# Rows 4 to 6 in halves, other sizes of the last loads, and another engine that clears the semaphores, in a streamed sum of squared differences

## The chip, the cores and the metric

The kernel runs on one core of one Trainium2 chip. The metric is device time in microseconds (us) of one execution. A profile of one execution is beside it: the instructions of every engine with start and duration, the DMA packets, and the times at which each transfer raised its semaphore (its landing).

## The reference

```python
def setup_inputs():
    batch, dim = 1024, 4096
    return {
        "x": np.random.randn(batch, dim).astype(np.float32),
        "y": np.random.randn(batch, dim).astype(np.float32),
        "axis": -1,
    }

def reference(x, y, axis):
    return np.sum((x - y) ** 2, axis=axis).astype(np.float32)
```

Two arrays of 16 MiB are read, and 1024 numbers are written.

## The kernel before

**Tiling.** Each of the 128 partitions holds 8 whole rows of x and of y, one after the other: 8 x 4096 = 32,768 columns (`xv`, `yv`, L60 and L61). The text calls them row 0 to row 7. X and Y have room in SBUF for six rows (`H = 6 * D`, L65), so columns from 24,576 on are put where rows 0 and 1 were (`home`, L97).

**Loads.** x comes in 6 pieces and y in 9, all issued by SP in one queue (`load`, L105 to L108), each with a semaphore of its own. The widths in columns stand in `xw` and `yw` (L72, L73). Two narrow pieces of y come last: the final `last` = 288 columns of row 7, and then the final `late` = 160 columns of row 3, which were left out of the first piece of y. `order` (L110 to L116) puts each piece of x ahead of the first piece of y that needs it. The first two loads are moved to the very start of the program (`early`). Loads up to column 24,576 are issued at once; the later ones wait on SP until the squares of rows 0 and 1 are done (L215) and are then all issued in a row (L219, L220). In the text x2 is the third piece of x, y8 the ninth piece of y; a column is one float on each of the 128 partitions.

**Work.** The loop at L191 goes through the pieces of y in the order of their loads. VectorE (DVE) waits until the piece and the x beside it have landed, and subtracts in place (`sub`, L168); a piece that crosses a row's end is cut there (`pieces_of`, L127). ScalarE (ACT) waits for the difference, squares it and adds it up along the row (`square`, L173). In the profile a square is two instructions, an ACTIVATE and an ACTIVATION_READ_ACCUMULATOR that writes the sum. Where a row is in several pieces, each sum goes into a column of `parts`, and `complete` (L181) adds them on DVE with a small TENSOR_REDUCE after waiting for ACT. Rows 0, 1, 2, 4 and 5 are squared whole and need none. Row 6 is in two parts and is completed after the fifth piece of y (`j == 4`, L221). Row 7 is in five parts and is completed last (L224). The late piece of row 3 (L197) is subtracted and then squared on DVE itself, in an instruction that starts from the partial sum that ACT left.

**End.** SP waits for all the sums and stores `results` (L226, L227). `close` then has SP clear the range of all the other semaphores (L44) while the store is under way, wait for the store's own semaphore, and take that semaphore back to zero in the same instruction (L45). Nothing follows it in the program.

Of the kernel before, what the change touches and what calls it, by code (L numbers as in the profile page):

```python
# [8 lines left out]
class Program:  # L9
# [27 lines left out]
        )  # L37
        self.entry[where:where] = taken

    def close(self, engine, stored, value):  # L40

        engine.sem_clear(range(self.sems[0].num, self.sems[-1].num + 1))  # L44
        engine.wait_ge(stored, value).then_inc(stored, -value)  # L45


def kernel(tc, x, y, axis, out):
    nc = tc.nc
    P = nc.NUM_PARTITIONS  # L50
    F32 = mybir.dt.float32
    Square = mybir.ActivationFunctionType.Square
    mult, add = mybir.AluOpType.mult, mybir.AluOpType.add

    B, D = x.shape
    R = B // P
    N = R * D


    xv = x.rearrange("(p r) d -> p (r d)", p=P)  # L60
    yv = y.rearrange("(p r) d -> p (r d)", p=P)  # L61
    ov = out.rearrange("(p r) -> p r", p=P)


    H = 6 * D  # L65
    X = nc.alloc_sbuf_tensor("X", [P, H], F32).ap()
    Y = nc.alloc_sbuf_tensor("Y", [P, H], F32).ap()
    results = nc.alloc_sbuf_tensor("results", [P, R], F32).ap()

    xw = [16384, 8192, 5568, 1824, 512, 288]  # L72
    yw = [16224, 8192, 2656, 2912, 928, 896, 512]  # L73
    late, last = 160, 288
    LATE = 3
    cut = (LATE + 1) * D - late
    assert sum(xw) == N and sum(yw) == N - late - last
    xs, c = [], 0
    for w in xw:
        xs.append((c, c + w))  # L80
        c += w
    ys, c = [], 0
    for w in yw:
        ys.append((c, c + w))
        c += w
        if c == cut:
            c += late
    ys += [(N - last, N), (cut, cut + late)]

    prog = Program(nc, tc)  # L90
    stored = nc.alloc_semaphore("stored")
    diffs = prog.semaphore("diffs")
    acts = prog.semaphore("acts")
    sums = prog.semaphore("sums")
    n = dict(diffs=0, acts=0, sums=0)

    def home(c0, c1):  # L97
        h0 = c0 % H
        return slice(h0, h0 + c1 - c0)


    landed_x, landed_y = [], []
    freed = []

    def load(landed, src, dst, name, c0, c1):  # L105
        sem = prog.semaphore("%s%d" % (name, len(landed)))
        nc.sync.dma_start(out=dst[:, home(c0, c1)], in_=src[:, c0:c1]).then_inc(sem, 16)  # L107
        landed.append(((c0, c1), sem))  # L108

    order = []  # L110
    have = 0
    for c0, c1 in ys:
        while have < c1:
            order.append((landed_x, xv, X, "x") + xs[len([o for o in order if o[3] == "x"])])
            have = order[-1][5]
        order.append((landed_y, yv, Y, "y", c0, c1))  # L116

    todo = list(order)
    for _ in range(2):
        load(*todo.pop(0))  # L120
    prog.early(mybir.EngineType.SP)
    while todo and todo[0][5] <= H:
        load(*todo.pop(0))


    row_parts = [[] for _ in range(R)]
    def pieces_of(c0, c1):  # L127
        pieces = []
        while c0 < c1:
            e = min(c1, (c0 // D + 1) * D)  # L130
            pieces.append((c0, e))
            c0 = e
        return pieces

    for c0, c1 in ys:
        for piece in pieces_of(c0, c1):
            row_parts[piece[0] // D].append(piece)
    parts, where = None, {}
    total = sum(len(p) for p in row_parts if len(p) > 1)
    parts = nc.alloc_sbuf_tensor("parts", [P, total], F32).ap()  # L140
    k = 0
    for r, p in enumerate(row_parts):
        for piece in p:
            where[piece] = parts[:, k : k + 1] if len(p) > 1 else results[:, r : r + 1]
            k += len(p) > 1
    first = {}
    k = 0
    for r, p in enumerate(row_parts):
        if len(p) > 1:
            first[r] = k  # L150
            k += len(p)

    def parts_of(r, m):
        return parts[:, first[r] : first[r] + m]

    seen_x = [0]

    def wait_loaded(c1, ysem):

        waits = []  # L160
        while seen_x[0] < len(xs) and xs[seen_x[0]][0] < c1:
            waits.append(seen_x[0])
            seen_x[0] += 1
        nc.vector.wait_ge(ysem, 16)
        for k in waits:
            nc.vector.wait_ge(landed_x[k][1], 16)

    def sub(c0, c1):  # L168
        a = X[:, home(c0, c1)]
        nc.vector.tensor_sub(out=a, in0=a, in1=Y[:, home(c0, c1)]).then_inc(diffs, 1)  # L170
        n["diffs"] += 1

    def square(c0, c1, acc):  # L173
        a = X[:, home(c0, c1)]
        nc.scalar.wait_ge(diffs, n["diffs"])
        nc.scalar.activation(out=a, in_=a, func=Square, accum_out=acc).then_inc(acts, 1)  # L176
        n["acts"] += 1

    squared = {}

    def complete(r):  # L181
        nc.vector.wait_ge(acts, squared[row_parts[r][-1]])
        nc.vector.tensor_reduce(  # L183
            out=results[:, r : r + 1],
            in_=parts_of(r, len(row_parts[r])),
            axis=mybir.AxisListType.X,
            op=add,
        ).then_inc(sums, 1)
        n["sums"] += 1

    for j, (c0, c1) in enumerate(ys):  # L191
        final = j == len(ys) - 1
        wait_loaded(c1, landed_y[j][1])
        for piece in pieces_of(c0, c1):
            sub(*piece)
            r = piece[0] // D
            if final:  # L197
                nc.vector.wait_ge(diffs, n["diffs"])
                nc.vector.tensor_tensor_reduce(  # L199
                    out=Y[:, home(*piece)],  # L200
                    in0=X[:, home(*piece)],
                    in1=X[:, home(*piece)],
                    scale=1.0,
                    scalar=parts_of(r, 1),
                    op0=mult,
                    op1=add,
                    accum_out=results[:, r : r + 1],
                ).then_inc(sums, 1)
                n["sums"] += 1
                continue  # L210
            square(*piece, where[piece])
            squared[piece] = n["acts"]
            if r in (0, 1):

                nc.sync.wait_ge(acts, n["acts"])  # L215
                while todo and todo[0][5] <= H + (r + 1) * D:
                    load(*todo.pop(0))
                if r == 1:
                    while todo:  # L219
                        load(*todo.pop(0))  # L220
        if j == 4:  # L221
            for r in (6,):
                complete(r)
    complete(7)  # L224

    nc.sync.wait_ge(sums, n["sums"])  # L226
    nc.sync.dma_start(out=ov, in_=results).then_inc(stored, 16)  # L227
    prog.close(nc.sync, stored, 16)


# [33 lines left out]
```

## Time and profile before

| what | value |
|---|---|
| median of 3 runs | 84.36 us (84.32 to 84.52) |
| the profiled execution's own time | 84.36 us |
| its span, first to last recorded instruction | 83.03 us (83.0 on the page) |
| outside the span | 1.33 us |
| DVE busy | 36.3 us (44%) in 18 instructions |
| ACT busy | 31.7 us (38%) in 27 instructions |
| DMA queue | 33.56 MB, busy for 95.2% of the span on 16 DMA engines |

The two compute engines are less than half busy, and the DMA queue nearly always. The page cuts the span into 40 slices and prints for each the busy share in tenths and the rate in GB/s. The chain of waits is followed back from the last instruction, and says at each step what released it. In the timeline each line gives the start, the duration, the engine, the source line, the operation with its shapes, and, in brackets, how long the engine stood idle before it and what ended that. A group such as "x3" runs from the start of the first to the end of the last of its instructions. SPq and POOLq are the sequencers of SyncE and GpSimd; their waits, drains and DMA issues aren't counted as busy.

### The profile page before, as it was taken

Reading aid. Unit: us, or ns where it says so; the run is one execution under the profiler, and the core shown is the slowest. Engines: PE = TensorE matmul, PEld = TensorE weight load, DVE = VectorE, ACT = ScalarE, POOL = GpSimd, SP = SyncE. Lnnn points to the kernel's source line nnn. Section 1 sums busy time; section 2 is a strip of 40 time slices with the busy share of each in tenths; the row PEclk is TensorE's granted clock in tenths of the full one; section 3 lists DMA queues with packets and bytes.
Section 4 is the critical chain, followed back from the end, with each engine's and each line's share of the span. In section 5 each row is a group of like instructions: output and inputs, shape, how many; then the busy total and the mean of one; then the engine's idle time right before and its main releaser. Section 6 shows DMA issues by size and latency. Waiting matters only on the chain.

```text
span 83.0 us, 109 instructions
## 1 busy us (share of the span) xinstructions
DVE 36.3 (44%) x18; ACT 31.7 (38%) x27; POOL 0.2 (0%) x4
## 2 busy tenths in 40 slices
DVE  0000000000000000000299999999099995979981
ACT  0500000000000000000001969798970796989991
POOL 0000000000000000000000000000000000000000
DMA  9299999929999997599799979979999999999940
GB/s 505 95 410 505 505 505 505 505 95 410 500 500 500 500 500 313 219 469 500 332 426 505 474 316 474 505 332 426 424 429 429 400 435 439 426 407 404 395 145 2
DMA packets 2304, 33.56 MB, mean 404 GB/s; under 512 B 384, under 2 KB 768, under 8 KB 1408
## 3 DMA queue, kind: packets, MB, share of 16 engines
q1 hardware_dynamic: 2304, 33.56, 95.2%
HBM read 33.55 MB, written 0.00 MB: 404 GB/s over the span
## 4 chain that ended last, share of the span: by engine, by line
DMA 68%; ACT 14%; DVE 14%; SPq 1%; issue 0%
DMA Y<-in_y_dram 68%; ACT X L176 14%; DVE X L170 14%; SPq L107 1%; DVE results L183 0%; SPq L215 0%
## 5 line engine op out<-in xcount | busy, mean ns | idle before, releaser
L170 DVE TENSOR_TENSOR X<-X,Y 128x4096 f32<-128x4096 f32 (+9 forms) x14 | 35.8, 2593 | 44.9 <-DMA Y<-in_y_dram 44.8
L176 ACT ACTIVATE X<-X 128x4096 f32<-128x4096 f32 (+8 forms) x13 | 29.7, 2288 | 47.7 <-DVE X L170 47.7
L176 ACT ACTIVATION_READ_ACCUMULATOR X<-X 128x1 f32 x13 | 2.4, 188 | 0.0
L176 ACT ACT_TABLE_LOAD x1 | 1.3, 1283 | 1.9 <-PEq L19 1.9
L183 DVE TENSOR_REDUCE results<-parts 128x1 f32<-128x2 f32 (+1 forms) x2 | 0.3, 154 | 0.2 <-ACT X L176 0.2
L199 DVE CUSTOM_DVE_ANT_0 Y<-X,parts 128x160 f32<-128x160 f32 x1 | 0.4, 385 | 0.0
L245 POOL MEMSET const-bfloat16-1.0<- 128x1 bf16 x1 | 0.1, 102 | 0.0
L245 POOL MEMSET const-uint8-127<- 128x1 uint8 x1 | 0.1, 102 | 0.0
L245 POOL MEMSET const-float32-0.0<- 128x1 f32 x1 | 0.1, 99 | 0.2 <-issue 0.2
L245 POOL MEMSET const-float32-1.0<- 128x1 f32 x1 | 0.1, 99 | 0.0
L199 DVE DVE_READ_ACCUMULATOR2_ANT results<- 128x1 f32 x1 | 0.1, 83 | 0.0
## 6 DMA issues: line engine op xcount, KB each, us to landing
Y<-in_y_dram SPq DMA_DIRECT2D x1, 8112.0 KB, 40.4
X<-in_x_dram SPq DMA_DIRECT2D x1, 4096.0 KB, 48.7
Y<-in_y_dram SPq DMA_DIRECT2D x1, 4096.0 KB, 58.0
X<-in_x_dram SPq DMA_DIRECT2D x1, 2784.0 KB, 13.4
Y<-in_y_dram SPq DMA_DIRECT2D x1, 1456.0 KB, 19.2
Y<-in_y_dram SPq DMA_DIRECT2D x1, 1328.0 KB, 16.2
X<-in_x_dram SPq DMA_DIRECT2D x1, 912.0 KB, 21.0
Y<-in_y_dram SPq DMA_DIRECT2D x1, 464.0 KB, 21.6
```

Of the source, the lines that this page charges most:

```text
L107: nc.sync.dma_start(out=dst[:, home(c0, c1)], in_=src[:, c0:c1]).then_inc(sem, 16)
L170: nc.vector.tensor_sub(out=a, in0=a, in1=Y[:, home(c0, c1)]).then_inc(diffs, 1)
L176: nc.scalar.activation(out=a, in_=a, func=Square, accum_out=acc).then_inc(acts, 1)
L183: nc.vector.tensor_reduce(out=results[:, r : r + 1], in_=parts_of(r, len(row_parts[r])), axis=mybir.AxisListType.X, op=add,).then_inc(sums, 1)
L199: nc.vector.tensor_tensor_reduce(out=Y[:, home(*piece)], in0=X[:, home(*piece)], in1=X[:, home(*piece)], scale=1.0, scalar=parts_of(r, 1), ...
L245: nc = _bacc.Bacc("TRN2", target_bir_lowering=False, num_devices=1)
```

## The change

Three things change. The pieces 1 to 4 of y, which hold rows 4, 5 and 6 and the first part of row 7, are subtracted and squared in two halves for each row that they touch. Rows 4 and 5 so have two partial sums each, and are completed beside row 6 at `j == 4`. The loads have other widths: the first piece of y is 32 columns wider, and the loads from row 6 on are 13 in place of 11 and narrower towards the end. And `close` no longer uses SP: GpSimd (POOL) waits for the store's semaphore, and then clears all the kernel's semaphores, that one among them. In the built program POOL's part is a drain that waits, followed by the clear.

```diff
-    def close(self, engine, stored, value):
-        engine.sem_clear(range(self.sems[0].num, self.sems[-1].num + 1))
-        engine.wait_ge(stored, value).then_inc(stored, -value)
+    def close(self, sem, value):
+        self.nc.gpsimd.wait_ge(sem, value)
+        self.nc.clear_and_free_semaphores(self.sems)
...
-    xw = [16384, 8192, 5568, 1824, 512, 288]
-    yw = [16224, 8192, 2656, 2912, 928, 896, 512]
-    late, last = 160, 288
+    xw = [16384, 8192, 5472, 1280, 960, 320, 160]
+    yw = [16256, 8192, 2624, 2784, 1344, 480, 480, 288]
+    late, last = 128, 192
     LATE = 3
+    halved = (1, 2, 3, 4)
...
-    stored = nc.alloc_semaphore("stored")
     diffs = prog.semaphore("diffs")
     acts = prog.semaphore("acts")
     sums = prog.semaphore("sums")
+    stored = prog.semaphore("stored")
...
-    def pieces_of(c0, c1):
+    def pieces_of(j, c0, c1):
         pieces = []
         while c0 < c1:
             e = min(c1, (c0 // D + 1) * D)
+            if j in halved:
+                h = (c0 + e) // 64 * 32
+                pieces.append((c0, h))
+                c0 = h
             pieces.append((c0, e))
             c0 = e
         return pieces
...
         if j == 4:
-            for r in (6,):
+            for r in (4, 5, 6):
                 complete(r)
     complete(7)

     nc.sync.wait_ge(sums, n["sums"])
     nc.sync.dma_start(out=ov, in_=results).then_inc(stored, 16)
-    prog.close(nc.sync, stored, 16)
+    prog.close(stored, 16)
```

The order of the last loads, with widths in columns, is:

| | order from row 6 on |
|---|---|
| before | x2 5568, y2 2656, y3 2912, x3 1824, y4 928, y5 896, x4 512, y6 512, x5 288, y7 288, y8 160 |
| after | x2 5472, y2 2624, y3 2784, x3 1280, y4 1344, x4 960, y5 480, y6 480, x5 320, y7 288, x6 160, y8 192, y9 128 |

On DVE there are 21 subtractions in place of 14 and 4 reductions in place of 2; on ACT 20 squares in place of 13; on SP 17 loads in place of 15.

More of the change, by code (lines that the diff above doesn't have):

```diff
@@ L133, in pieces_of @@
         return pieces
-    for c0, c1 in ys:
-        for piece in pieces_of(c0, c1):
+    for j, (c0, c1) in enumerate(ys):
+        for piece in pieces_of(j, c0, c1):
             row_parts[piece[0] // D].append(piece)
@@ L193 @@
         wait_loaded(c1, landed_y[j][1])
-        for piece in pieces_of(c0, c1):
+        for piece in pieces_of(j, c0, c1):
             sub(*piece)
```

## The prediction

> **What bounds the kernel now.** I read the page first, then the chain of waits, then the timeline of the last 5 us.
>
> ```profile
> DMA  9299999929999997599799979979999999999940
> ## 4 chain that ended last, share of the span: by engine, by line
> DMA 68%; ACT 14%; DVE 14%; SPq 1%; issue 0%
> ```
>
> The loads run to slice 39 of 40, and only the end is not theirs. The chain of waits says what hangs behind them:
>
> ```profile
> 70.12 2.94 DVE X L170
> ...
> 73.07 8.29 ACT X L176 x14
> ...
> 81.39 0.16 DVE results L183
> ```
>
> From 73.07 to 81.37 ACT squares without a pause: the tail's bound is ACT running late, not the last load. ACT was late since the whole-row squares of rows 4 and 5. The timeline's end:
>
> ```profile
> 79.28 1.43 DVE L170 TENSOR_TENSOR X<-X,Y 128x512 f32<-128x512 f32 x3 [0.16 <-DMA Y<-in_y_dram]
> 79.29 0.94 ACT L176 ACTIVATE X<-X 128x896 f32<-128x896 f32 x1
> ...
> 80.22 0.61 ACT L176 ACTIVATE X<-X 128x512 f32<-128x512 f32 x1
> ...
> 80.84 0.43 ACT L176 ACTIVATE X<-X 128x288 f32<-128x288 f32 x1
> 81.06 0.08 DVE L199 DVE_READ_ACCUMULATOR2_ANT results<- 128x1 f32 x1
> 81.17 0.19 ACT L176 ACTIVATION_READ_ACCUMULATOR X<-X 128x1 f32 x1
> 81.39 0.16 DVE L183 TENSOR_REDUCE results<-parts 128x1 f32<-128x5 f32 x1 [0.25 <-ACT X L176]
> 81.58 0.35 SPq L227 DMA_DIRECT2D out_dram<-results  x1
> ```
>
> DVE is through at 81.14 and waits 0.25 us for ACT. So at most 0.25 is won by a punctual ACT alone; more needs an earlier DVE. The store is issued at 81.58 and lands at 83.00 (1.42 later); SP's last wait ends the span at 83.03. The clear is hidden meanwhile:
>
> ```profile
> L44 SPq EVENT_SEMAPHORE_RANGE_CLEAR  x1: 62/62/62, 82.0 to 82.0; - x1
> L45 SPq EVENT_SEMAPHORE  x1: 17/17/17, 83.0 to 83.0; - x1
> ```
>
> I work from the profiled execution, 84.36 us: span 83.03 and 1.33 outside it, which I hold equal. It is also the median of the 3 runs.
>
> **Prices.** DVE, start to start without a wait between: 4.341 us for 4096 columns (60.327 to 64.670 unrounded: 4.343), 1.576 for 1440, so 0.077 + 0.00104 per column. ACT: 2.416 for 2656, 0.613 for 512, so 0.182 + 0.000841 per column. A difference reaches ACT 0.12 after DVE could start its next subtraction (64.67 to 64.79). A landing releases DVE 0.02 later.
>
> **Part 1, the loads.** Each of 16 DMA engines takes 8 of a load's 128 rows. Packets of 65,536 bytes take 2,418 ns, those of 640 bytes 32 ns: 0.0368 ns a byte, and with 4 x 8 bytes a column 1.177 ns a column. Between y1's landing (60.30) and y8's (80.20) lie 16,544 columns, 19.47 us by that price; the remaining 0.43 over 11 loads is 0.04 a load. After: y1 lands at 60.34 (32 columns more in y0), then 16,512 columns, 19.43, and 13 loads, 0.51: the last landing is 80.28, 0.08 later. By loads: y2 69.99, y3 73.32, y4 76.47, y5 78.23, y6 78.83, y7 79.61, y8 80.08, y9 80.27. Bounds of a load's fixed cost: 0.01 (y8 before: 0.20 after y7, of which its 160 columns are 0.19) and that whole 0.20; two extra loads cost 0.02 to 0.40. I take 0.08, since eleven rows give it.
>
> ```profile
> Y<-in_y_dram SPq DMA_DIRECT2D x1, 80.0 KB, 15.4
> ```
>
> This is y8, issued 15.4 us ahead of its landing. SP's issues are held up (4.87 us at most, y7), so two more could end about 10 us after the present 67.56, which is before their data's turn at 80; the store behind them on SP waits until 81 anyway.
>
> [...]
>
> **Part 2, the halves.** Seven more subtractions (0.077 each, 0.54) and squares (0.182 each, 1.27) lie mostly in idle time: before, DVE waits 1.03 for y2 and 0.57 for y3, ACT 3.02 for row 4. DVE after: rows 4 and 5 start at 60.36, 62.57, 64.78, 66.99 and end by 69.2, before y2. Row 6: 70.01 and 71.45; y3's four pieces 73.34 to 76.55, y4's two to 78.10. There the three completions stand, in front of y5 on DVE; each costs 0.065 (77.972 to 78.037 before). Row 6's last square starts at 75.14 and is done at 76.05, so none waits. y5 78.30, y6 78.87, y7 79.63 (landing), y8 80.11 (landing), y9 80.38.
>
> ACT then follows each half: row 5's second half starts at 69.32 and ends at 71.3 (72.83 before), row 6 71.57 and 73.01, y3 from 74.30, y4 77.44 and 78.22, y5 78.99, y6 79.58, y7 80.16, y8 80.58. That one takes 0.182 + 0.161, and 0.107 more until the accumulator is in (81.170 + 0.187 + 0.010 before): 81.03.
>
> DVE's own end: y9's 128 columns from 80.38, next possible start 80.59, its difference back at itself 0.12 later (80.71), the multiply 0.143 + 0.133 until the accumulator read at 80.99 (before 80.749 to 81.059 for 160), 0.065 to the next: 81.05. So both engines meet at 81.05 where before ACT alone gave 81.39: **minus 0.34**. The store is issued at 81.24 and lands at 82.66. The eight partial sums instead of five cost the last reduction nothing I can see (149 and 158 ns for 2 and 5).
>
> [...]
>
> **Part 3, the close.** SP ends with the store's issue. POOL has waited since 1.81 with nothing behind but the clear, and this now stands after the landing. The trace before has no clear on POOL; the nearest rows:
>
> ```profile
> L19 POOLq DRAIN  x2: 34/38/41, 1.2 to 1.5; - x2
> ```
> ```profile
> L245 POOLq DRAIN  x1: 181/181/181, 0.3 to 0.3; - x1
> ```
>
> Waking 0.017 as SP's, a drain 0.04, 0.08 between sequencer instructions (POOL's waits at 1.383 and 1.462), a clear 0.062 as SP's: 0.20, less SP's 0.034: **plus 0.17**. Below: 0.045, if drain and gap overlap the wait. Above: POOL's three rounds of start-up barriers, 1.06 to 1.81, 0.75 us for its whole routine, if ending on POOL costs something outside the span too. I take 0.17, nearest to the sequencer rows.
>
> Sum: 84.36 - 0.34 + 0.17 = **84.19 us** (82.86 span).
>
> **Rivals.**
> - Cheap close (0.045): 84.36 - 0.34 + 0.05 = 84.07. For it: the clear itself is 62 ns on SP. Against: POOL's drains take 4 to 5 times SP's 7 ns.
> - Loads dear: 0.40 for two, 0.32 more than I took: 84.51. Against: the rows between x2 and y8 show it nowhere.
> - The halves don't bring ACT forward (if DVE's additional work pushes every difference back): with whole pieces and the new loads the same sum gives ACT 81.44 and the reduction 81.46, +0.07: 84.36 + 0.07 + 0.17 = 84.60.
> - Slower: POOL as last engine costs its 0.75: 84.36 - 0.34 + 0.75 = 84.77. It decides from 0.34 on. For it: POOL idles from 1.81 and its end is hidden now, whatever it costs; against: its single instructions take 17 to 41 ns.
>
> **Numbers.** What a measurement can tell here is about 0.3%, 0.25 us: below 84.11 is faster, above 84.61 slower. Chances: forecast 0.45 (84.05 to 84.40), cheap close 0.17, loads dear 0.12, halves void 0.08, dear close 0.18. Faster: cheap close and 0.06 of the forecast, 0.23. Slower: dear close and nearly half of halves void, 0.21. Within: 0.56. The range leaves out most of the dear close, so 83.95 to 84.65.
>
> **What would show it.** Right: the last reduction starts at 81.0 to 81.1, ACT idles between squares after 71, the last load lands near 80.28, POOL's clear ends some 0.2 after the store's landing. Wrong: ACT busy without gap from 73 on; DVE unable to start y7 at its landing; the last landing beyond 80.4; or the time outside the span grown above 1.33, which would be POOL's end.

## The result: 0.6% slower, and the span unchanged

| | before | after |
|---|---|---|
| median of 4 runs | 84.42 us (84.32 to 84.52) | 84.91 us (84.87 to 85.03) |
| ratio after to before, 95% interval | | 1.0060 (1.0043 to 1.0078) |
| profiled execution, own time | 84.36 | 84.87 |
| its span | 83.03 | 83.04 |
| outside the span | 1.33 | 1.83 |

The change costs half a microsecond, and the last row alone holds it: the first and last instruction of the profile are as far apart as before. The profile of after follows, in the order of the lines shown before the change. First its page:

```profile
DMA  9289999948999997499899969989999999999940
...
DMA 64%; SPq 17%; DVE 12%; ACT 4%; issue 1%
```

The loads still run to slice 39. In the chain ACT has gone from 14% to 4%. (The 17% of SPq are SP's held-up load issues, 4.78 us at most, which the chain now follows back; SP issues its last load by 70.88, and that load lands at 80.37, so they delay nothing.) The chain of waits of after ends so (start, duration, what):

```profile
80.19 0.02 issue
80.21 0.57 DVE X L177 x2
80.78 0.03 issue
80.81 0.35 DVE Y L206
81.16 0.01 DVE results L206
81.17 0.14 DVE results L190
```

Where 8.29 us of ACT stood, there now stands DVE from the landing of y8 on. The timeline of after at the same place:

```profile
78.34 2.42 DVE L177 TENSOR_TENSOR X<-X,Y 128x480 f32<-128x480 f32 x5
...
80.67 0.35 ACT L183 ACTIVATE X<-X 128x192 f32<-128x192 f32 x1
...
80.92 0.19 ACT L183 ACTIVATION_READ_ACCUMULATOR X<-X 128x1 f32 x1
81.08 0.08 DVE L206 DVE_READ_ACCUMULATOR2_ANT results<- 128x1 f32 x1
81.14 0.16 DVE L190 TENSOR_REDUCE results<-parts 128x1 f32<-128x8 f32 x1
81.33 0.35 SPq L234 DMA_DIRECT2D out_dram<-results  x1
```

ACT's last sum is in at 81.11, just ahead of DVE's; the last reduction carries no idle time in brackets, where 0.25 us of waiting for ACT stood. It starts at 81.14, 0.25 ahead of before, in an execution whose loads landed 0.17 later (80.37 against 80.20). Then comes the close (line, duration min/median/max in ns, first and last start in us):

```profile
L46 POOLq DRAIN  x1: 88/88/88, 82.8 to 82.8; - x1
L46 POOLq EVENT_SEMAPHORE_RANGE_CLEAR  x1: 157/157/157, 82.9 to 82.9; - x1
```

The store lands at 82.74, the clear ends at 83.04: 0.30 us where SP needed 0.03. That eats the 0.25 of the tail. The other 0.50 lies after the last instruction, where the page shows nothing. The traces' record of semaphore updates reaches further. Its first update behind the span's end comes 0.14 after it before, at 83.171, and 0.53 after it in the changed kernel, at 83.564. The last update of semaphore 96 stands at 83.627 before, 0.60 after the span's end, and at 84.146 after, 1.11 after the span's end. Counted from the first instruction, the execution's own time is up 0.73 and 0.72 later. So 0.39 of the half microsecond lies between the program's last instruction and the first update behind it, and all of it ahead of that update of semaphore 96.

### The profile page after: what moved, and what is told of

The parts are those of the page before. It is cut to its first block, busy times and chain, and to the rows that moved or that the text cites. A ratio compares the mean times of both kernels' runs of the same rounds, so it can differ in the third digit from the quotient of the medians.

```text
span 83.0 us, 135 instructions
## 1 busy us (share of the span) xinstructions
DVE 36.8 (44%) x27; ACT 33.4 (40%) x41; POOL 0.2 (0%) x4
## 4 chain that ended last, share of the span: by engine, by line
DMA 64%; SPq 17%; DVE 12%; ACT 4%; issue 1%
DMA Y<-in_y_dram 64%; SPq L109 17%; DVE X L177 11%; ACT X L183 4%; DVE Y L206 0%; DVE results L190 0%; SPq L222 0%; DVE results L206 0%
## 5 line engine op out<-in xcount | busy, mean ns | idle before, releaser
L177 DVE TENSOR_TENSOR X<-X,Y 128x2048 f32<-128x2048 f32 (+10 forms) x21 | 36.2, 1779 | 44.4 <-DMA Y<-in_y_dram 44.3
L183 ACT ACTIVATE X<-X 128x2048 f32<-128x2048 f32 (+9 forms) x20 | 31.2, 1560 | 45.8 <-DVE X L177 45.7
L183 ACT ACTIVATION_READ_ACCUMULATOR X<-X 128x1 f32 x20 | 3.7, 187 | 0.0
```

## The experiments

My theory was that POOL, when it is the engine that ends last, costs the half microsecond. The rivals were the larger program (135 instructions in the trace against 109), and a clear that comes after the landing, on whatever engine. Each run is compared with runs of the kernel before on its own chip; "outside" is the profiled execution's time less its span. The diffs show the lines that matter; "..." stands for lines that add or move a semaphore, change the call of `close`, or put SP's close back.

**The new close alone**, on the kernel before.

```diff
-        engine.sem_clear(range(self.sems[0].num, self.sems[-1].num + 1))
-        engine.wait_ge(stored, value).then_inc(stored, -value)
+        self.nc.gpsimd.wait_ge(sem, value)
+        self.nc.clear_and_free_semaphores(self.sems)
...
```

> The kernel before with the new close alone. In the changed kernel the close took 0.26 us more inside the span (0.30 from landing to end against 0.03) and the time outside the span was 0.50 longer (1.83 against 1.33). Theory POOL-last (whatever POOL does last after the store costs 0.5 outside the span): 84.42 + 0.26 + 0.50 = 85.2, outside 1.83. Theory larger program (135 instructions against 109 cost the 0.5): 84.42 + 0.26 = 84.7, outside 1.33. Theory late clear (a clear of semaphores after the landing costs 0.5 outside, on any engine): 85.2, as POOL-last.

Measured: 85.29 against 84.57, ratio 1.0088 (1.0068 to 1.0109), outside 1.84. The larger program falls: this one has the loads and pieces of before.

**Halves and loads alone**: the changed kernel with SP's close.

```diff
-        self.nc.gpsimd.wait_ge(sem, value)
-        self.nc.clear_and_free_semaphores(self.sems)
+        engine.sem_clear(range(self.sems[0].num, self.sems[-1].num + 1))
+        engine.wait_ge(stored, value).then_inc(stored, -value)
...
```

> The changed kernel with the close of before on SP: halves and new loads alone. POOL-last and late clear: 84.91 - 0.76 = 84.15, outside 1.33, the last reduction near 81.14 as in the changed kernel. Larger program: 84.91 - 0.26 = 84.65, outside 1.83.

Measured: 84.22 against 84.57, ratio 0.9959 (0.9943 to 0.9974), outside 1.33, the last reduction at 81.15:

```profile
81.15 0.16 DVE L190 TENSOR_REDUCE results<-parts 128x1 f32<-128x8 f32 x1
```

By its ratio it is the fastest kernel of this study, ahead of before and of after. The effects of the two runs, +0.88% and -0.41%, add up to +0.47%; the whole change gave +0.60% (0.43 to 0.78).

**Only the wait on POOL**, with SP's clear under the store.

```diff
         engine.sem_clear(range(self.sems[0].num, self.sems[-1].num + 1))
-        engine.wait_ge(stored, value).then_inc(stored, -value)
+        self.nc.gpsimd.wait_ge(stored, value).then_inc(stored, -value)
```

> The kernel before; SP still clears under the store, but the wait for the store that takes its semaphore back to zero is on POOL. POOL-last: 84.42 + 0.5 = 84.9, outside 1.83, span within 0.1 of before. Late clear and larger program: 84.4 to 84.5, outside 1.33.

Measured: 85.06 against 84.57, ratio 1.0071 (1.0046 to 1.0097), outside 1.88. The lines of this run's close:

```profile
L44 SPq EVENT_SEMAPHORE_RANGE_CLEAR  x1: 57/57/57, 82.1 to 82.1; - x1
L45 POOLq EVENT_SEMAPHORE  x1: 17/17/17, 83.1 to 83.1; - x1
```

POOL does nothing but a 17 ns wait, as long as SP's own, and the half microsecond is there.

**The clear after the landing, on SP**, on the kernel before.

```diff
-        engine.sem_clear(range(self.sems[0].num, self.sems[-1].num + 1))
-        engine.wait_ge(stored, value).then_inc(stored, -value)
+        self.nc.sync.wait_ge(sem, value)
+        self.nc.sync.sem_clear(range(self.sems[0].num, self.sems[-1].num + 1))
...
```

> The kernel before with SP waiting for the store first and then clearing all semaphores, the store's among them. POOL-last and larger program: only the clear comes onto the path, 0.05 of gap and 0.06: 84.42 + 0.1 = 84.5, outside 1.33. Late clear: 84.5 + 0.5 = 85.0, outside 1.83.

Measured: 84.57 against 84.57, ratio 1.0002 (0.9990 to 1.0013), outside 1.32. From landing to end 0.08 us instead of 0.03: a serial clear on SP is worth 0.05, too little to see in the time. The late clear falls as a cause: on SP it costs nothing outside the span, and the run with only the wait on POOL had the half microsecond without it.

**The clear on POOL, but under the store**, with SP's wait last.

```diff
-        engine.sem_clear(range(self.sems[0].num, self.sems[-1].num + 1))
+        go = self.semaphore("go")
+        engine.wait_ge(self.sems[2], 1).then_inc(go, 1)
+        self.nc.gpsimd.wait_ge(go, 1)
+        self.nc.gpsimd.sem_clear(range(self.sems[0].num, self.sems[-1].num + 1))
         engine.wait_ge(stored, value).then_inc(stored, -value)
```

> The kernel before, with the clear on POOL while the store is under way (SP signals POOL after issuing the store), and SP's wait last as before. POOL ends about 0.5 or more ahead of SP. If what costs is POOL ending last: same as before within 0.1, outside 1.33. If any late work on POOL costs: 0.5 longer, outside 1.8.

Measured: 84.44 against 84.40, ratio 1.0009 (0.9995 to 1.0024), outside 1.33. POOL's clear took 138 ns against the 62 of SP's in the kernel before, and cost nothing that shows: POOL ended at 82.12 and SP at 82.99.

```profile
L47 POOLq EVENT_SEMAPHORE_RANGE_CLEAR  x1: 138/138/138, 82.0 to 82.0; - x1
```

**The last wait on ACT, on PE, on DVE.** The kernel before, three times:

```diff
-        engine.wait_ge(stored, value).then_inc(stored, -value)
+        self.nc.scalar.wait_ge(stored, value).then_inc(stored, -value)
```

with `scalar`, `tensor` and `vector`.

> As the run in which POOL held the last wait, but ACT holds it. Theory POOL alone (its own end of program is longer, 1.84 to 1.88 outside the span against 1.33 for SP): same time as before within 0.1, outside 1.3 to 1.4. Theory any-engine-but-SP (the store's issuer should end last): 0.5 longer, outside 1.8.

> As above, the last wait on PE. POOL alone: same as before within 0.1, outside 1.3 to 1.4. Any-engine-but-SP: 0.5 longer, outside 1.8.

> As the run with the wait on ACT, the last wait on DVE. POOL alone: same as before within 0.1, outside 1.3 to 1.4. Any-engine-but-SP: 0.5 longer, outside 1.8.

Both theories missed: it is neither POOL alone nor all but SP alike, but a ladder.

| engine that ends last | outside | ratio to before |
|---|---|---|
| SP (before) | 1.33 | |
| DVE | 1.46 | 1.0032 (1.0020 to 1.0043) |
| ACT | 1.50 | 1.0017 (0.9994 to 1.0040) |
| PE | 1.66 | 1.0036 (1.0022 to 1.0051) |
| POOL (wait only) | 1.88 | 1.0071 (1.0046 to 1.0097) |

The ratio orders DVE and ACT the other way than the time outside, with intervals that overlap: those two aren't told apart by the ratio. Each row's time outside is that of one profiled execution; the four other runs that SP ends with its wait for the store give 1.33 to 1.34, and the three that POOL ends 1.83 to 1.88.

What makes the ladder isn't shown: no instruction is recorded behind the last one of the program. The run with POOL's clear under the store agrees with an ending of POOL's that is as long there, and hidden: counted from POOL's end at 82.12, the 1.83 to 1.88 are up at 83.95 to 84.00, ahead of the execution's 84.32.

**SP goes on after POOL has ended.**

```diff
-        engine.sem_clear(range(self.sems[0].num, self.sems[-1].num + 1))
+        most = range(self.sems[0].num, self.sems[-1].num + 1)
+        engine.sem_clear(most)
         engine.wait_ge(stored, value).then_inc(stored, -value)
+        engine.sem_clear(most).then_inc(go, 1)
+        self.nc.gpsimd.wait_ge(go, 1).then_inc(go, -1)
+        for _ in range(4):
+            engine.sem_clear(most)
...
```

> The kernel before; after the store has landed SP signals POOL, whose last wait ends then, and SP goes on with four more clears, about 0.1 each, so SP ends some 0.4 after POOL. If each engine's ending has its own length beyond its last instruction and the longest decides (POOL about 1.85, SP 1.33), SP's 0.4 is hidden in POOL's 0.5: 84.40 + 0.1 (signal) + 0.52 = 85.0, and 1.4 to 1.5 outside the span that SP now ends. If the endings add up or POOL's cost comes only when it is the last of all: 84.40 + 0.1 + 0.4 = 84.9 with 1.33 outside, or 85.4 with 1.85 outside.

Measured: 85.08 against 84.48, ratio 1.0074 (1.0060 to 1.0089). Its lines:

```profile
L48 POOLq EVENT_SEMAPHORE  x1: 17/17/17, 83.2 to 83.2; - x1
L50 SPq EVENT_SEMAPHORE_RANGE_CLEAR  x4: 53/53/58, 83.2 to 83.5; - x4
```

POOL's wait ends at 83.18 and the span, with SP, at 83.51. Counted from the first instruction, the execution's time is up at 85.06: 1.88 after POOL, exactly as in the run where POOL was last, and 1.56 after SP. SP's 0.33 us are hidden. I read this as endings that run side by side, of which the one that is through last decides; here it is POOL's, though SP's instructions end later.

**New loads without the halves**, with the close on SP.

```diff
-    halved = (1, 2, 3, 4)
+    halved = ()
...
-            for r in (4, 5, 6):
+            for r in (6,):
...
```

> The new widths of the loads without the halves, and the close of before on SP. By the sum that gave 81.05 for both together, whole pieces leave ACT late: its last sum at 81.44, the last reduction at 81.46 against 81.39: 0.07 over before, and ACT busy without a pause in the last 5 us. If the new widths alone carry the gain (rival: smaller last pieces shorten the end), as with both: 0.35 under before.

Measured: 84.57 against 84.48, ratio 1.0018 (1.0005 to 1.0031). Its chain of waits and the end of its timeline:

```profile
72.94 8.51 ACT X L183 x16
```
```profile
81.00 0.35 ACT L183 ACTIVATE X<-X 128x192 f32<-128x192 f32 x1
...
81.48 0.16 DVE L190 TENSOR_REDUCE results<-parts 128x1 f32<-128x6 f32 x1 [0.33 <-ACT X L183]
```

ACT is busy from 72.94 on without a pause, and DVE waits 0.33 for it: the last reduction at 81.48, 0.09 over before, where the sum said 0.07.

**Halves without the new loads**, with the close on SP.

```diff
-    xw = [16384, 8192, 5472, 1280, 960, 320, 160]
-    yw = [16256, 8192, 2624, 2784, 1344, 480, 480, 288]
-    late, last = 128, 192
+    xw = [16384, 8192, 5568, 1824, 512, 288]
+    yw = [16224, 8192, 2656, 2912, 928, 896, 512]
+    late, last = 160, 288
...
```

> The halves of rows 4 to 6 on the old widths, and the close of before on SP. By the sum, ACT keeps up until 78 but is late again through 896 and 512 columns whole: the last reduction at 81.49, 0.10 over before. If the halves alone carry the gain, 0.35 under before.

Measured: 84.63 against 84.48, ratio 1.0017 (1.0008 to 1.0025). Its chain of waits, and its timeline:

```profile
79.52 2.09 ACT X L183 x6
```
```profile
79.52 0.95 ACT L183 ACTIVATE X<-X 128x896 f32<-128x896 f32 x1 [0.26 <-DVE X L177]
...
81.63 0.16 DVE L190 TENSOR_REDUCE results<-parts 128x1 f32<-128x7 f32 x1 [0.33 <-ACT X L183]
```

Here ACT had caught up: at 79.52 it waits for DVE. But then it has 896, 512 and 288 columns to square in one piece each, and is late again; the last reduction is at 81.63, in an execution that landed its last load 0.17 later than before. Each half of the remedy alone costs some 0.1 us (0.09 and 0.15), and both together win 0.35: the halves let ACT catch up by 78, the narrow last pieces keep it there.

## Why the prediction was wrong

**The tail was right.** The forecast took 0.34 off for the halves and loads; the run that holds them alone gives 0.35 (84.57 less 84.22, 0.22 to 0.48 by the interval). From the last landing to the last reduction the sum said 0.78 (80.27 to 81.05); after shows 0.77 (80.37 to 81.14), before 1.19. The landings between y1 and y9 were to take 19.93 us and took 19.96. Of the 0.09 by which the whole tail stood later than the sum, 0.07 was there at y1 (60.41 against 60.34). That is within the scatter of executions: in the ten profiled kernels with the old widths y1 landed between 60.26 and 60.50.

**The close inside the span was too small.** I took 0.17 above SP's; it was 0.26. The drain took 88 ns where I put 40 from the start-up drains, and the clear 157 where I put SP's 62. (POOL's start-up drains, 34 to 41 ns, are five to six times SP's 7, not the four to five that the prediction says.) That alone would have left 84.36 - 0.25 + 0.26, no change.

**The step that failed** is "1.33 outside it, which I hold equal". The time outside goes by the engine that ends last (1.33 with SP, 1.46 to 1.66 with DVE, ACT and PE, 1.83 to 1.88 with POOL), and the change hands that place from SP to POOL: plus 0.50, of which 0.39 lies ahead of the first semaphore update behind the last instruction (0.14 after SP's, 0.53 after POOL's). The prediction's last sign of being wrong, a time outside the span grown above 1.33, is the one that came. The rival "dear close" had the direction, the place and nearly the size: 0.75 priced, 0.76 found (0.26 inside, 0.50 outside). It was given 0.18, and its time of 84.77 was left out of the range, though 0.75 was my own upper bound for that cost; a range that took the bound in would still have missed the time by 0.14. Its price came from POOL's start-up barriers, a row that has no shown link to the ending, so the closeness is luck, and no proof of that mechanism.

**What I argued from** was the length of POOL's single instructions, 17 to 41 ns. The run with only the wait on POOL shows why this could not answer: the instruction took 17 ns there too, and its cost stood behind it. What would have helped is that the trace has a record behind the span: updates of semaphores that go on from 0.14 us after SP's end, so the time outside isn't empty. How long it would be behind POOL could not be read there: POOL was idle from 1.81 on.

**What stays open** is why the time outside is 1.83 to 1.88 behind POOL's last instruction, where it is 1.33 behind SP's, 1.46 behind DVE's, 1.50 behind ACT's and 1.66 behind PE's. No instruction is recorded there. Whether a kernel can shorten POOL's part wasn't tried.

## What to carry to other kernels

Let the engine with the shortest ending execute the program's last instruction: here SP, which was worth 0.5 us against POOL. Work on POOL that ended early enough was free here: a clear that ended 0.87 ahead of SP cost nothing that shows, and a wait that ended 0.33 ahead was not early enough. My estimate for the limit is 0.50 to 0.55, POOL's 1.83 to 1.88 outside less SP's 1.33, if the endings run side by side. Read the span and the time outside it apart: a change can win in the one and lose in the other, and the busy times show only the first. When an engine is late because of large pieces, cut the pieces up to the end: here cutting the early ones alone, or narrowing the last ones alone, lost some 0.1 us each.

## What the runs showed of the hardware

- The execution's time was 1.32 to 1.34 us longer than the span when SP had the last instruction, 1.46 with DVE, 1.50 with ACT, 1.66 with PE and 1.83 to 1.88 with POOL; with POOL's last instruction 0.33 ahead of SP's it was up 1.88 after POOL's.
- The first semaphore update behind the last instruction came after 0.14 us where SP had it (before) and after 0.53 us where POOL had it (after); the last update of semaphore 96 came 0.60 and 1.11 us after it.
- Clearing a range of semaphores took 138 and 157 ns on POOL, and 53 to 65 ns on SP.
- In after, the 13 loads from row 6 on were issued 9.9 to 21.9 us ahead of their landings, and the DMA engines were busy for 97 to 100% of each stretch between 60 and 80 us: they took 0.53 us above 1.177 ns a column, 0.04 each, as the 11 of before did.
